# A sum of two accumulator halves: copied half by half, or copied whole and added in SBUF

## The chip, the cores and the metric

The kernel runs on one core of a Trainium2 chip, with its engines TensorE (PE, with its weight loads PEld), VectorE (DVE), ScalarE (ACT), GpSimd (POOL) and the queue of SyncE (SP). The metric is the device time of one execution, in microseconds (us), and the median over the runs is what counts.

## The reference

One decoder block over 256 tokens of width 2048 and 256 memory vectors, all in fp32. Three parts follow one another, each with a norm before and after it and a residual: a mixer of three recurrent branches, a cross attention with 4 heads, and a convolutional FFN.

```python
h = rms_norm(x, norm_mix_pre)
z = h @ w_in                                  # columns of all three branches and their gates
o_a = gated_delta_rule(q, k, v, g, beta)      # 8 heads of 128; q, k, v after a causal conv (4 taps) and silu
y_a = (rms_norm(o_a) * silu(dz)) @ w_dn_out
o_b = gla_chunked(gq, gk, gv, log_a)          # 4 heads, chunks of 64
y_b = (rms_norm(o_b) * silu(gr)) @ w_gla_out
y_s = gelu(s5_ssm(su, ...))                   # 64 groups, state 64, a scan over the tokens
y_c = glu_a * sigmoid(glu_b)                  # glu_a, glu_b = split(y_s @ w_s5_glu)
x = x + rms_norm((g_a * y_a + g_b * y_b + g_c * y_c) @ w_mix_out)
x = x + rms_norm(cross_attention(rms_norm(x), rms_norm(mem)))
gate, up = split(rms_norm(x) @ w_ffn_up)      # 2 x 5632 columns
x = x + rms_norm((gelu(causal_conv(gate)) * up) @ w_ffn_down)
```

## The kernel before

**Products in high and low halves.** Every fp32 operand is split into a rounded half (high) and the rest (low), and a product is made of three passes: high by high, high by low, low by high. `load_w` (lines 199 to 207) loads a weight tile of two 128-row blocks and 512 columns (`raw`, SP's queue), ScalarE casts it to `whi` (L206), and VectorE subtracts to get `wlo` (L206 too). `raw` has four buffers, `whi` and `wlo` three each, so the casts run at most three weight tiles ahead of TensorE.

**Two ways of multiplying.** `proj` keeps features on the partitions: the activations hold their high half in columns 0 to 255 and their low half in columns 256 to 511, so one matmul of 512 columns with `whi` (L222) makes two of the three products side by side in one PSUM bank, and one of 256 columns with `wlo` (L226) adds the third into the first half. A slab is 512 columns of weights, with four accumulators and eight weight tiles for K = 2048. At its end each accumulator holds two halves that have to be added: this is `total` (lines 209 to 213), which the evacuation function of a slab calls for each accumulator. There are 152 such calls: 8 for the S5 input, 24 for the DeltaNet q, k and v, 8 for GLA's q and k, 16 for the two output gates (`gated`), 8 in the cross attention, and 88 in the FFN's upward product. `proj_tok` keeps tokens on the partitions, with two accumulators (L282, L286) and no `total`.

**PSUM.** Five of the eight banks rotate as accumulators (`ps_acc`), three as small tiles (`ps_mx`). A slab of four accumulators therefore begins with one free bank, and its second to fourth accumulators need the banks that the slab before has just filled.

**Rows.** `total` and the evacuations work in rows of 256 columns from a pool (`row`, tag `r1`, 8 buffers in the mixer); rows of 512 columns (`row2`, tag `r2`, 2 buffers) hold the mixer's gates, which go out to DRAM by DMA from GpSimd's queue. In the convolutions (`conv_silu`) the sum is read by ScalarE (L386) and three times by VectorE (L388), in the gates (`gated`) by ScalarE (L626), in the FFN by VectorE's product with the norm and then by ScalarE (L1447) and VectorE (L1449).

**What sets the order.** The Python code emits slabs in order and, between weight tiles, pieces of background work from generators (`pump`): the DeltaNet core, GLA, the S5 expansions (L921), its scan of three small VectorE operations per token (L931 to L933) and its outputs (L946). A scheduler then places all instructions on their engines by its own timeline; `load_w` stands in a high priority. Each engine executes its queue in the order so made, and a change of one helper moves what surrounds it.

Of the kernel before, what the change touches and what calls it, by code (L numbers as in the profile page):

```python
# [9 lines left out]
F32 = mybir.dt.float32  # L10
# [8 lines left out]
P = 128  # L19
T = 256  # L20
# [3 lines left out]
NW = 512  # L24
# [64 lines left out]
class Net:  # L89
# [117 lines left out]
        return hi, lo  # L207

    def total(self, acc, out=None):
        r = self.row() if out is None else out  # L210
        self.nc.scalar.copy(r, acc[:, T:2 * T])  # L211
        self.nc.vector.tensor_add(r, r, acc[:, 0:T])  # L212
        return r

    def tile_passes(self, accs, hi, lo, rhs, g, KT, n):
# [94 lines left out]
    def open_main(self):  # L310
        c = self.ctx
        self.main_stack = ExitStack()
        self.sp = self.main_stack.enter_context(self.pool("sp"))
        self.s16 = self.main_stack.enter_context(self.pool("s16", bufs=1))
        self.s8 = self.main_stack.enter_context(self.pool("s8", bufs=3))
        self.s4 = self.main_stack.enter_context(self.pool("s4", bufs=6))
        self.t1 = self.main_stack.enter_context(self.pool("t1", bufs=8))
        self.jv = self.sp.tile([P, P], F32, name="jv")
        self.ja = self.sp.tile([P, T], F32, name="ja")

# [10 lines left out]
        return self.t1.tile([P, T], F32, name="r1", tag="r1")  # L331

    def row2(self):
        return self.t1.tile([P, NW], F32, name="r2", tag="r2", bufs=2)

    def small_cols(self, small, ab_in):
        nc = self.nc
# [1235 lines left out]
```

## Time and profile before

| | us |
|---|---|
| median of 3 runs | 1924.62 |
| lowest and highest run | 1921.52, 1929.48 |
| the profiled execution | 1925.81 |
| its span, first to last instruction | 1924.0 |
| TensorE busy | 1873.0 |
| VectorE busy | 1415.4 |
| ScalarE busy | 959.6 |

TensorE's mean granted clock over the span is 0.991 of full speed. In the profile, a group of instructions is written as line, engine, operation, output and inputs, shape and count, then the busy time in us, the mean of one in ns, and the engine's idle time before them with what ended it. In a table of stretches, each engine has its busy time and its number of instructions, in the order PE, PEld, DVE, ACT, POOL; then come the granted clock, the DMA's share and GB/s. In a list of waits, a row gives the waiting engine with its tile and line, what it waited for, the sum in us, how often, and the longest. In the timeline, a row starts with its start and duration, and a bracket holds the idle time of the engine before it.

The program begins with the S5 input, then DeltaNet's k, q and v with their convolutions (to about 240 us), the mixer's gates with the DeltaNet core behind them, GLA's q, k and v (about 430 to 545), the DeltaNet gate (from 545), the other gates, the output products and the mix, the cross attention (about 1060 to 1160), and from about 1200 the FFN.

### The profile page before, as it was taken

The page shows a single profiled execution, that of the slowest core. Times are in us where ns is not written, and L with a number is a line of the kernel's source. Part 1 is how long each engine was busy: PE and PEld are TensorE (multiplying, and loading weights), DVE is VectorE, ACT ScalarE, POOL GpSimd, SP SyncE. Part 2 cuts the span into 40 slices and gives each one's busy share as a digit, 9 for nine tenths or more (in the row PEclk, how much of TensorE's full clock was granted, in tenths as well). Part 3 has the DMA queues.
Part 4 walks back from the last instruction along what each step waited for, and adds up shares of the span by engine and source line. Part 5 has one row for each costly group of instructions (what it writes and reads, how often), then busy time and mean ns, then how long its engine had stood idle before and what let it go on. Part 6 is the DMA issues. An engine that isn't in the chain of part 4 may idle for free.

```text
span 1924.0 us, 28133 instructions
## 1 busy us (share of the span) xinstructions
PE 1873.0 (97%) x10440; PEld 1573.9 (82%) x10440; DVE 1415.4 (74%) x2719; ACT 959.6 (50%) x1428; POOL 67.4 (4%) x117
## 2 busy tenths in 40 slices
PE   7999999999999999999999997999999999999997
PEld 6788888777877688888888986888888888888886
DVE  6878999997469999977666755777666677644445
ACT  5655544443564444444455654655555555544442
POOL 0000012020000000000000000000000000000000
PEclk9989999999999999999999998999999999999999
DMA  7544477674445575666587544766666656766664
GB/s 256 164 130 155 155 210 234 195 253 140 133 121 162 182 225 177 213 216 216 186 266 225 174 153 140 219 182 184 201 188 188 189 183 186 228 215 198 198 195 131
DMA packets 107482, 363.93 MB, mean 189 GB/s; under 512 B 12320, under 2 KB 20896, under 8 KB 106832
## 3 DMA queue, kind: packets, MB, share of 16 engines
q1 hardware_dynamic: 97696, 328.32, 55.3%
q0 software_dynamic: 9648, 33.81, 5.3%
q8 instruction: 82, 1.34, 0.3%
q14 instruction: 56, 0.46, 0.1%
HBM read 350.47 MB, written 11.61 MB: 188 GB/s over the span
## 4 chain that ended last, share of the span: by engine, by line
PE 89%; DVE 6%; ACT 2%; issue 1%; DMA 1%; DVEq 0%; SPq 0%; POOL 0%; ACTq 0%; POOLq 0%
PE acc L282 28%; PE acc L222 27%; PE acc L286 14%; PE acc L226 14%; DVE wlo L206 2%; PE mx L921 2%; DMA raw<-in 1%; ACT whi L206 1%; DVE r L388 1%; PE mx L183 0%; PE mx L640 0%; DVE mm L931 0%; DVE f L518 0%; PE mx L946 0%; DVE X L933 0%
## 5 line engine op out<-in xcount | busy, mean ns | idle before, releaser
L206 DVE TENSOR_TENSOR wlo<-raw,whi 128x1024 fp32r<-128x1024 f32 (+1 forms) x632 | 752.3, 1195 | 388.3 <-ACT whi L206 366.6
L206 ACT CAST whi<-raw 128x1024 fp32r<-128x1024 f32 (+1 forms) x632 | 645.6, 1029 | 672.1 <-PE acc L282 339.1
L222 PE MATMUL acc<-aa,whi 128*128 128x512 f32 x2224 | 620.7, 398 | 10.7 <-DVE r L212 8.3
L222 PEld LDWEIGHTS acc<-aa,whi 128*128 128x128 f32 x2224 | 383.6, 190 | 63.9 <-issue 9.8
L226 PEld LDWEIGHTS acc<-aa,wlo 128*128 128x128 f32 x2224 | 345.4, 191 | 59.1 <-DVE wlo L206 11.5
L226 PE MATMUL acc<-aa,wlo 128*128 128x256 f32 x2224 | 362.1, 283 | 7.6 <-DVE wlo L206 7.4
L282 PE MATMUL acc<-whi,aa 128*128 128x512 f32 (+1 forms) x1408 | 346.5, 383 | 0.0
L282 PEld LDWEIGHTS acc<-whi,aa 128*128 128x128 f32 x1408 | 255.3, 188 | 53.3 <-issue 2.3
L286 PE MATMUL acc<-wlo,aa 128*128 128x512 f32 (+1 forms) x704 | 191.5, 383 | 2.8 <-DVE wlo L206 2.7
L286 PEld LDWEIGHTS acc<-wlo,aa 128*128 128x128 f32 x704 | 127.9, 188 | 31.5 <-DVE wlo L206 6.6
L282 PE MATMUL acc<-whi,ach 128*128 128x512 f32 x352 | 137.0, 389 | 0.0
L282 PE MATMUL acc<-whi,acl 128*128 128x512 f32 x352 | 136.9, 389 | 0.0
L931 DVE TENSOR_TENSOR mm<-M,X 128x128 f32<-128x128 f32 x254 | 98.7, 389 | 5.1 <-ACT X L925 0.3
L286 PE MATMUL acc<-wlo,ach 128*128 128x512 f32 x352 | 95.4, 389 | 0.0
L282 PEld LDWEIGHTS acc<-whi,ach 128*128 128x128 f32 x352 | 66.1, 188 | 13.7
L286 PEld LDWEIGHTS acc<-wlo,ach 128*128 128x128 f32 x352 | 66.1, 188 | 13.7
L282 PEld LDWEIGHTS acc<-whi,acl 128*128 128x128 f32 x352 | 66.0, 188 | 13.7
L933 DVE TENSOR_TENSOR X<-X,s__868 128x64 f32<-128x64 f32 x255 | 71.6, 281 | 4.8
L282 PE MATMUL acc<-whi,mgx 128*128 128x512 f32 x256 | 64.3, 391 | 0.1
L211 ACT COPY r<-acc 128x256 f32<-128x256 f32 x143 | 49.6, 362 | 27.3 <-PE acc L222 26.8
L932 DVE TENSOR_TENSOR s__868<-mm 128x64 f32<-128x64 f32 x255 | 56.5, 222 | 4.5
L212 DVE TENSOR_TENSOR r<-r,acc 128x256 f32<-128x256 f32 x143 | 57.0, 413 | 0.9 <-ACT r L211 0.9
(439 smaller groups left out, 1558.5 us busy)
## 6 DMA issues: line engine op xcount, KB each, us to landing
raw<-in SPq DMA_DIRECT2D x600, 512.0 KB, 4.0
raw<-in SPq DMA_DIRECT2D x32, 256.0 KB, 2.7
gd<-r POOLq DMA_DIRECT2D x24, 256.0 KB, 4.4
f<-gd POOLq DMA_DIRECT2D x12, 512.0 KB, 4.8
f<-Rd POOLq DMA_DIRECT2D x4, 512.0 KB, 7.2
f<-in POOLq DMA_DIRECT2D x4, 512.0 KB, 4.5
gp<-in POOLq DMA_DIRECT2D x8, 256.0 KB, 4.7
xn<-in POOLq DMA_DIRECT2D x1, 2048.0 KB, 11.0
```

Source lines behind the costliest of these rows:

```text
L206: self.last = (nc.scalar.copy(hi, raw), self.seq(lambda: nc.vector.tensor_sub(lo, raw, hi.bitcast(F32))))
L211: self.nc.scalar.copy(r, acc[:, T:2 * T])
L212: self.nc.vector.tensor_add(r, r, acc[:, 0:T])
L222: nc.tensor.matmul(accs[m], hi[:, kk, ms[m]], xs[kk].rearrange("p c s -> p (c s)"), start=ks[kk] == 0, stop=ks[kk] == KT - 1)
L226: nc.tensor.matmul(accs[m][:, :T], lo[:, kk, ms[m]], xs[kk][:, 0, :], start=False, stop=False)
L282: nc.tensor.matmul(accs[t], xs[kk][i][:, t * P:(t + 1) * P], hi[:, kk, :], start=ks[kk] == 0 and i == 0, stop=False)
L286: last[:] = [nc.tensor.matmul(accs[t], xs[kk][0][:, t * P:(t + 1) * P], lo[:, kk, :], start=False, stop=ks[kk] == KT - 1)]
L388: nc.vector.scalar_tensor_tensor(c[:, d:], raw[:, :T - d], w[:, j, 3 - d:4 - d], c[:, d:], op0=ALU.mult, op1=ALU.add)
L921: nc.tensor.matmul(ps[:, n, c, :], self.Bl[c][rs, ft, :], su[rs, ft, tk], start=True, stop=True, tile_position=(32 * q, 0))
L931: nc.vector.tensor_mul(m, self.M, prev[:, None].broadcast_to([P, 2, 2, 32]))
L932: nc.vector.tensor_add(s, m[:, :, 0, :], m[:, :, 1, :])
L933: nc.vector.tensor_add(X[:, :, :, t], X[:, :, :, t], s)
```

## The change

`total` copies the whole accumulator, 512 columns, into a row of 512, and VectorE adds the row's two halves in SBUF. Before, ScalarE copied the second half alone and VectorE added the first half to it out of PSUM. Rows of 512 get three buffers in place of two, and the mixer's rows of 256 six in place of eight. The pools of the cross attention and of the FFN, which had no rows of 512, now hold three of them too.

```diff
     def total(self, acc, out=None):
-        r = self.row() if out is None else out
-        self.nc.scalar.copy(r, acc[:, T:2 * T])
-        self.nc.vector.tensor_add(r, r, acc[:, 0:T])
+        both = self.row2()
+        self.nc.scalar.copy(both, acc)
+        r = both[:, :T] if out is None else out
+        self.nc.vector.tensor_add(r, both[:, :T], both[:, T:])
         return r
...
-        self.t1 = self.main_stack.enter_context(self.pool("t1", bufs=8))
+        self.t1 = self.main_stack.enter_context(self.pool("t1", bufs=6))
...
     def row2(self):
-        return self.t1.tile([P, NW], F32, name="r2", tag="r2", bufs=2)
+        return self.t1.tile([P, NW], F32, name="r2", tag="r2", bufs=3)
```

No line on the order of the passes is changed. The scheduler makes a new order from it, though: on TensorE the high passes of a weight tile now stand more often in one run of eight, with the eight low ones behind them. Below `L212` the changed kernel's line numbers are larger by one (its add is L213). Three places of the new order matter further on.

**First place: the first slab of the DeltaNet gate, ScalarE and VectorE.** `r_5473` and its like are rows, `acc` an accumulator, `f_5634` and `f_5711` tiles of GLA. ScalarE before:

```order
L206 CAST whi<-raw 128x1024 x2
L211 COPY r_5473<-acc 128x256
L206 CAST whi<-raw 128x1024
L704 ACTIVATE f_5634<-f_5634 128x1024
L704 ACTIVATE f_5711<-f_5711 128x1024
L626 ACTIVATE r_5472<-r_5473 128x256
L628 ACTIVATE r_5477<-r_5472 128x256
L211 COPY r_5481<-acc 128x256
L626 ACTIVATE r_5480<-r_5481 128x256
L628 ACTIVATE r_5485<-r_5480 128x256
L211 COPY r_5503<-acc 128x256
```

And now:

```order
L206 CAST whi<-raw 128x1024 x2
L211 COPY r_5477<-acc 128x512
L211 COPY r_5485<-acc 128x512
L211 COPY r_5507<-acc 128x512
L206 CAST whi<-raw 128x1024
L705 ACTIVATE f_5638<-f_5638 128x1024
L705 ACTIVATE f_5715<-f_5715 128x1024
L627 ACTIVATE r_5476<-r_5477 128x256
L206 CAST whi<-raw 128x1024 x2
L629 ACTIVATE r_5481<-r_5476 128x256
L627 ACTIVATE r_5484<-r_5485 128x256
L211 COPY r_5515<-acc 128x512
```

The first three copies stand in a row, ahead of GLA's exponentials, and the fourth behind three more casts. VectorE's adds before:

```order
L701 TENSOR_TENSOR f_5711<-f_5258 128x512
L702 TENSOR_TENSOR f_5711<-f_5258 128x512
L212 TENSOR_TENSOR r_5473<-r_5473,acc 128x256
L721 COPY_PREDICATED f_5291<-cst,mx 128x512
L206 TENSOR_TENSOR wlo<-raw,whi 128x1024
```

And now:

```order
L702 TENSOR_TENSOR f_5715<-f_5262 128x512
L703 TENSOR_TENSOR f_5715<-f_5262 128x512
L213 TENSOR_TENSOR r_5477<-r_5477 128x256
L213 TENSOR_TENSOR r_5485<-r_5485 128x256
L213 TENSOR_TENSOR r_5507<-r_5507 128x256
L722 COPY_PREDICATED f_5295<-cst,mx 128x512
L206 TENSOR_TENSOR wlo<-raw,whi 128x1024
```

Three adds stand where one stood, and none of them reads an accumulator.

**Second place: GLA's q and k, ScalarE and TensorE.** `r_4559` to `r_4571` are the rows of q's four accumulators, `f_4305` the buffer that L1182 scales them into, which the DeltaNet core reads until it is done; L587, L604 and L617 are parts of that core. ScalarE before:

```order
L211 COPY r_4559<-acc 128x256
L211 COPY r_4563<-acc 128x256
L211 COPY r_4567<-acc 128x256
L206 CAST whi<-raw 128x1024
L211 COPY r_4571<-acc 128x256
L587 COPY f_3901<-mx 128x512
```

And now, eight casts (one slab) later than there:

```order
L206 CAST whi<-raw 128x1024
L588 COPY f_4137<-mx 128x512
L1183 ACTIVATE f_4305<-r_4559 128x256
L1183 ACTIVATE f_4305<-r_4563 128x256
L1183 ACTIVATE f_4305<-r_4567 128x256
L211 COPY r_4571<-acc 128x512
L605 COPY f_2160<-mx 128x512
```

The fourth copy has moved from the end of q's slab to the end of k's. TensorE at the end of k's slab, before (L282 and L286 are the passes of the v product, L577 to L602 the core's):

```order
L577 MATMUL mx<-f_3757,f_837 64x128 x8
L226 MATMUL acc<-aa,wlo 128x256 x2
L222 MATMUL acc<-aa,whi 128x512
L282 MATMUL acc<-whi,aa 128x512 x4
L286 MATMUL acc<-wlo,aa 128x512 x2
L282 MATMUL acc<-whi,aa 128x512 x4
L286 MATMUL acc<-wlo,aa 128x512 x2
L584 MATMUL mx<-f_2160,f_3467 64x128 x8
L599 MATMUL mx<-f_3757,f_837 64x128 x2
L282 MATMUL acc<-whi,aa 128x512 x4
L286 MATMUL acc<-wlo,aa 128x512 x2
L602 MATMUL mx<-f_4137,f_2583 64x128 x2
```

And now:

```order
L227 MATMUL acc<-aa,wlo 128x256 x2
L223 MATMUL acc<-aa,whi 128x512
L578 MATMUL mx<-f_3757,f_837 64x128 x8
L585 MATMUL mx<-f_2160,f_3467 64x128 x8
L600 MATMUL mx<-f_3757,f_837 64x128 x2
L603 MATMUL mx<-f_4137,f_2583 64x128 x2
```

The three batches of v passes are gone from between the core's products; the first v pass now stands behind all of them and behind the S5 products that follow.

**Third place: the second slab of the DeltaNet gate, TensorE.** L640 are the products that scale the core's output, L718 GLA's level products, one level in each run of 16; `mx` is a small PSUM tile. Before:

```order
L640 MATMUL mx<-r_5518,f_2160 128x64 x8
L718 MATMUL mx<-f_5416 64x64 x16
L222 MATMUL acc<-aa,whi 128x512 x8
L226 MATMUL acc<-aa,wlo 128x256 x8
L222 MATMUL acc<-aa,whi 128x512 x4
L718 MATMUL mx<-f_5553 64x64 x16
L718 MATMUL mx<-f_5634 64x64 x16
L222 MATMUL acc<-aa,whi 128x512 x4
L226 MATMUL acc<-aa,wlo 128x256 x8
L718 MATMUL mx<-f_5711 64x64 x16
```

And now:

```order
L641 MATMUL mx<-r_5522,f_2160 128x64 x8
L719 MATMUL mx<-f_5420 64x64 x16
L227 MATMUL acc<-aa,wlo 128x256 x2
L223 MATMUL acc<-aa,whi 128x512 x2
L719 MATMUL mx<-f_5557 64x64 x16
L719 MATMUL mx<-f_5638 64x64 x16
L719 MATMUL mx<-f_5715 64x64 x16
L719 MATMUL mx<-f_4305 64x64 x16
L227 MATMUL acc<-aa,wlo 128x256 x2
```

The level products have come together, in the last weight tile of the slab, where they were spread over three tiles.

## The prediction

> **What bounds the kernel now.** I read the page's first part, then the waits of TensorE, then the engines by stretches of the program, then the timeline where the longest waits lie.
>
> ```profile
> PE 1873.0 (97%) x10440; PEld 1573.9 (82%) x10440; DVE 1415.4 (74%) x2719; ACT 959.6 (50%) x1428; POOL 67.4 (4%) x117
> ...
> 240.00:432.00 192.00, 189.24 (x1047) 153.31 (x1046) 186.37 (x393) 83.85 (x100) 31.48 (x54) 1.00 0.73 223
> ...
> 584.00:816.00 232.00, 232.00 (x1336) 188.10 (x1337) 221.16 (x542) 111.22 (x163) 10.89 (x18) 1.00 0.63 195
> ...
> 1200.00:1680.00 480.00, 479.72 (x2739) 419.96 (x2738) 338.14 (x542) 260.51 (x403) 1.27 (x2) 1.00 0.63 194
> ```
>
> TensorE (PE, first pair of busy time and count in each stretch) is busy 97% of the span, and from 1200 to 1680 us, the upward FFN product, it idles 0.28 us. All of its passes stay, so nothing is to be had there: 88 of the 152 calls of `total` lie in that product. The gain can only be what TensorE still waits for, 51 us in all, or what it loses at half clock. Its waits name the accumulator:
>
> ```profile
> PE acc L222 <- DVE r L212: 8.3, 5, 2.5
> PE acc L226 <- DVE wlo L206: 7.7, 8, 2.9
> ...
> PE acc L222 <- DVE s__868 L932: 1.7, 3, 1.3
> ```
>
> A first pass into an accumulator (L222) waits for the add in `total` (L212), since that add is the last reader of an earlier accumulator in the same bank. The third row is the same wait under another name: at its longest, the add ends 0.15 us before TensorE goes on.
>
> ```profile
> 197.25 0.41 DVE L212 TENSOR_TENSOR r<-r,acc 128x256 f32<-128x256 f32 x1
> ...
> 197.81 0.70 PE L222 MATMUL acc<-aa,whi 128*128 128x512 f32 x2 [1.26 <-DVE s__868 L932]
> ```
>
> So 8.3 + 1.7 = 10.0 us are spent waiting for that add. Half of it lies in one place, the first slab of the DeltaNet gates:
>
> ```profile
> 569.59 0.37 ACT L211 COPY r<-acc 128x256 f32<-128x256 f32 x1 [3.50 <-PE acc L222]
> ...
> 574.81 0.41 DVE L212 TENSOR_TENSOR r<-r,acc 128x256 f32<-128x256 f32 x1
> ...
> 575.28 0.73 PE L222 MATMUL acc<-aa,whi 128*128 128x512 f32 x2 [2.45 <-DVE r L212]
> ...
> 576.65 0.35 ACT L211 COPY r<-acc 128x256 f32<-128x256 f32 x1
> ...
> 579.82 0.41 DVE L212 TENSOR_TENSOR r<-r,acc 128x256 f32<-128x256 f32 x1
> ...
> 580.38 0.70 PE L222 MATMUL acc<-aa,whi 128*128 128x512 f32 x2 [2.50 <-DVE r L212]
> ```
>
> The copy is done at 569.96, but the add stands in VectorE's queue behind GLA work and starts 4.9 us later. The next accumulator's copy stands on ScalarE behind the first one's gate, and the second wait follows. TensorE then loses time a second way, its granted clock (the number behind the last engine's pair):
>
> ```profile
> 116.00:120.00 4.00, 3.19 (x21) 2.23 (x21) 4.00 (x5) 1.51 (x3) 0.00 (x0) 1.00 0.67 178
> 120.00:124.00 4.00, 4.00 (x26) 3.55 (x25) 2.75 (x6) 2.38 (x5) 0.00 (x0) 0.55 0.67 221
> 124.00:128.00 4.00, 4.00 (x14) 3.16 (x14) 1.41 (x4) 1.67 (x4) 0.00 (x0) 0.50 0.00 0
> 128.00:132.00 4.00, 4.00 (x18) 3.60 (x19) 1.21 (x5) 1.64 (x4) 0.00 (x0) 0.50 0.00 0
> 132.00:136.00 4.00, 4.00 (x19) 3.38 (x19) 3.48 (x19) 1.21 (x3) 0.00 (x0) 0.75 0.01 2
> ...
> 580.00:584.00 4.00, 3.62 (x14) 2.95 (x16) 3.86 (x15) 2.19 (x6) 0.00 (x0) 0.65 0.00 1
> 584.00:588.00 4.00, 4.00 (x38) 3.54 (x38) 3.01 (x8) 2.45 (x4) 0.00 (x0) 0.93 0.02 4
> ```
>
> Around 120 the loss is (0.45 + 0.50 + 0.50 + 0.25) x 4 = 6.8 us; after the two gate waits it is (0.35 + 0.07) x 4 = 1.7 us.
>
> **The change, part by part.** What it does to the instructions is told by these rows:
>
> ```profile
> L212 DVE TENSOR_TENSOR r<-r,acc 128x256 f32<-128x256 f32 x143 | 57.0, 413 | 0.9 <-ACT r L211 0.9
> L211 ACT COPY r<-acc 128x256 f32<-128x256 f32 x143 | 49.6, 362 | 27.3 <-PE acc L222 26.8
> L1443 DVE TENSOR_TENSOR r<-r,rfr 128x256 f32<-128x256 f32 x88 | 35.1, 420 | 0.7
> L1154 ACT ACTIVATE r<-acc 128x512 f32<-128x512 f32 x24 | 14.1, 594 | 11.1 <-PE acc L286 11.1
> ```
>
> *The copy* doubles to 512 columns: the nearest row with that shape out of PSUM is L1154, 594 ns, so 152 x (594 - 362) = 35 us more on an engine that is 50% busy. In the FFN stretch above ScalarE idles 219 of 480 us, and the 88 copies there add 20: nothing. *The add* now reads SBUF only: L1443 has this shape, 420 against 413 ns, so 1 us over 152 calls, hidden in the same way. *The release*: the bank is free when ScalarE has copied, and VectorE's queue no longer stands between. At the gate slab the three first copies now stand in a row (first place of the order above); the one that TensorE wants at 572.83 would end at 569.59 + 0.59 = 570.2. In the convolution slabs the same: -10.0 us, bounds -5 (the half before 240 us is given back, see the rivals) and -10. *The clock* after the gate waits goes with them: -1.7, bounds 0 and -1.7.
>
> *The stretch at half clock around 120.* Ahead of it stand short waits, then the S5 expansions (L921), small products between the passes.
>
> ```profile
> 99.90 0.70 PE L222 MATMUL acc<-aa,whi 128*128 128x512 f32 x2 [1.07 <-DVE r L212]
> ...
> 118.03 0.51 PE L226 MATMUL acc<-aa,wlo 128*128 128x256 f32 x2 [0.65 <-DVE wlo L206]
> ```
>
> The expansions' number stays, their neighbours change. Bounds 0 and -6.8. The trace's other short falls cost 1.7 us; if what stays lies midway between 1.7 and 6.8, it costs 4.3, so -2.5. [...]
>
> *The rows.* The copy now takes a row of 512 columns, of which there are three, shared with the gates' rows. At GLA's q and k (second place) the first three rows are held until the DeltaNet core has left the buffer that L1182 writes; the fourth copy, 8 casts later now, keeps the bank that the v product needs.
>
> ```profile
> 472.53 1.08 PE L282 MATMUL acc<-whi,aa 128*128 128x512 f32 x4
> 473.90 1.07 PE L282 MATMUL acc<-whi,aa 128*128 128x512 f32 x4
> 475.36 1.09 PE L584 MATMUL mx<-f,f 64*64 64x128 f32 x16
> 476.74 1.20 PE L282 MATMUL acc<-whi,aa 128*128 128x512 f32 x4
> ...
> 480.65 1.34 ACT L1182 ACTIVATE f<-r 128x256 f32<-128x256 f32 x4 [3.57 <-PE mx L599]
> ...
> 486.35 1.20 PE L282 MATMUL acc<-whi,aa 128*128 128x512 f32 x4
> ```
>
> Three batches of v passes run here before L1182 can, each 1.37 us from start to start (472.53 to 473.90): 4.1 us of work that now waits. Without them the core's own products move up: L584's input is ready some 1.8 us before it runs, and what follows it is held by the third batch for about 1 us more, so about 2.7. So +1.4 us, bounds 0 and +4.1.
>
> *GLA's level products* (third place) now come in one block behind the gates' products, which hold two of the three small PSUM tiles until their rows are ready.
>
> ```profile
> 592.21 0.74 DVE L721 COPY_PREDICATED f<-cst,mx 128x512 f32<-128x512 int32 x1
> 592.83 1.23 DVE L727 TENSOR_TENSOR f<-f 128x1024 f32<-128x1024 f32 x1
> ...
> 593.54 2.09 PE L718 MATMUL mx<-f 128*64 128x64 f32 x64
> ```
>
> Each needs the tile that an L721 frees. Two L721 and the L727 between them are 2.7 us of VectorE against the 2.1 us of two levels on TensorE (these 64 instructions): about 0.6, and a little more at the transposes behind; I take +1.0, bounds 0 and +4, a wait of this size at each of the last levels.
>
> The profiled execution took 1925.81 us, 1.8 beyond its span of 1924.0, and 1.2 above the median of 1924.62. Sum: 1925.8 - 10.0 - 1.7 - 2.5 + 1.4 + 1.0 = 1914.0, and 1.2 less against the median: **1913 us**, 0.6% faster.
>
> **The rivals.** *The half-clock stretch stays whole*, or comes at another place: 1913 + 2.5 to 4 = 1916 to 1917. For it: the L921 are all still there. *It is gone*, because the waits for the add ahead of it are gone as they are in the gate slab: 1913 - 4.3 = 1909. For it: the fall at 580 came right after two such waits. Against it: the 1.07 us lies 20 us ahead of this one, and the wait for wlo at 118 stays. [...]
>
> *The wait becomes one for the low halves.* VectorE is busy 186 of 192 us from 240 and 221 of 232 from 584; if TensorE comes earlier, it may wait there for wlo, as it already does for 7.7 us. Then the 5 us before 240 and some of the gate's 5 come back, and the clock loses as before: 1922 to 1924, no change. Against it: VectorE has 5.6 and 10.8 us to spare there, and TensorE had no wait at all from 584 to 816.
>
> *Slower: the fourth copy blocks ScalarE.* With three rows for four accumulators, the fourth copy waits for the first row, and the casts of the weights stand behind it in ScalarE's queue.
>
> ```profile
> 1316.38 0.48 DVE L1449 SCALAR_TENSOR_TENSOR r<-r,vec,r 128x254 f32<-128x254 f32 x1
> ...
> 1317.98 0.36 ACT L211 COPY r<-acc 128x256 f32<-128x256 f32 x1
> ...
> 1320.04 2.00 ACT L206 CAST whi<-raw 128x1024 fp32r<-128x1024 f32 x2 [0.60 <-PE acc L222]
> ```
>
> Today the first row's last reader ends at 1316.86, 1.1 us ahead of the fourth copy, and the next cast still waits 0.6 us for TensorE, two weight tiles ahead (5.6 us: a tile is 16 passes, and 2739 passes fill the 480 us above). It decides from about 5 us of delay a slab; 1 us beyond that in 20 FFN slabs would make 1913 + 20 = 1933.
>
> **How the numbers follow.** The forecast (1908 to 1918 with its own spread) 0.42; stretch whole or elsewhere 0.20; stretch gone 0.18; waits for wlo 0.12; slower 0.08. A measurement can tell 0.5%, 9.6 us, so faster means below 1915.0: 0.29 of the first, 0.06 of the second, all of the third, 0.53, and 0.01 from the fourth. Slower by over 0.5% comes from the last, 0.08, and 0.01 from the fourth; no change is the rest, 0.37. Range: the lower end is all bounds at their best, 1925.8 - 18.5 - 1.2 = 1906, and 2 of the 7.7 us for wlo, 1904; the upper end takes in the fourth case, 1923.
>
> **What would show it.** Right: no row "PE acc <- DVE" for the add, and less than 2 us for the copy in its stead; L211 at about 590 ns and its add at about 420; no wait and full clock in the gate slab; 1 to 4 us of new idle time before the v product; the FFN still without idle time. Wrong: more than 8 us for wlo, a half-clock stretch of 7 us or more, or waits of "ACT r L211" for VectorE followed by late casts.

## The result: 1909 us, 0.85% faster

| | before | after |
|---|---|---|
| median of 4 runs, us | 1926.27 | 1909.32 |
| lowest and highest | 1921.52, 1929.48 | 1908.72, 1909.99 |
| the profiled execution, its span | 1925.81, 1924.0 | 1909.99, 1907.8 |
| TensorE busy, idle in the span | 1873.0, 51.0 | 1863.1, 44.7 |

The ratio of the runs is 0.9915, with an interval of 0.9902 to 0.9929. The forecast was 1913 us, with a range of 1904 to 1923 and 0.54 for faster by over 0.5%. Time and direction came out inside it, but two terms of the sum were wrong in size, on opposite sides, and what one of them was taken from differs from one execution to the next.

In the profile after, the waits of TensorE come first. A row gives the waiting engine with its tile and line, what it waited for, the sum in us, how often, and the longest.

```profile
PE acc L223 <- DVE xset L1061: 10.6, 2, 10.2
PE acc L227 <- DVE wlo L206: 6.9, 5, 2.9
PE mx L183 <- DVE xn L1289: 5.9, 1, 5.9
PE acc L287 <- DVE wlo L206: 3.2, 8, 0.8
PE mx L947 <- issue: 1.8, 1, 1.8
PE mx L585 <- DVE f L580: 1.3, 1, 1.3
PE mx L922 <- DVE rsoy L196: 0.9, 1, 0.9
PE mx L719 <- DVE f L722: 0.7, 1, 0.7
```

The waits for the add (8.3 and 1.7 us before) are gone, and none for the copy stands in their place. Waits for the low halves are 6.9 us on L227, 7.7 before on the same line; they did not take over. Four new rows stand at L947, L585, L922 and L719. The groups show what the copy and the add cost now (busy us, mean ns, idle time before them):

```profile
L211 ACT COPY r<-acc 128x512 f32<-128x512 f32 x151 | 87.0, 582 | 35.4 <-PE acc L223 28.0 <-DVE f L1090 0.5
L213 DVE TENSOR_TENSOR r<-r 128x256 f32<-128x256 f32 x144 | 59.9, 420 | 4.8 <-ACT r L211 4.4
```

The copy takes 582 ns (the estimate was 594), the add 420 (420). By stretches of the profile after, with the busy time and count of PE, PEld, DVE, ACT and POOL, then the granted clock:

```profile
0.00:240.00 240.00, 227.44 (x1353) 197.54 (x1354) 204.29 (x512) 146.45 (x226) 5.70 (x13) 0.99 0.60 186
432.00:488.00 56.00, 51.73 (x462) 40.95 (x459) 45.78 (x128) 26.37 (x57) 2.09 (x4) 0.97 0.39 116
545.00:640.00 95.00, 94.06 (x715) 72.20 (x714) 91.85 (x208) 52.81 (x86) 5.43 (x8) 1.00 0.53 164
...
56.00:60.00 4.00, 4.00 (x18) 3.39 (x18) 4.00 (x8) 3.55 (x8) 0.00 (x0) 0.69 0.72 240
...
120.00:124.00 4.00, 4.00 (x33) 3.28 (x32) 2.79 (x5) 2.57 (x7) 0.00 (x0) 1.00 0.84 233
124.00:128.00 4.00, 4.00 (x33) 3.62 (x32) 2.99 (x7) 3.67 (x8) 0.00 (x0) 1.00 0.39 160
...
580.00:584.00 4.00, 4.00 (x38) 3.36 (x38) 3.90 (x9) 1.64 (x2) 0.00 (x0) 1.00 0.67 207
...
1200.00:1680.00 480.00, 480.00 (x2720) 420.41 (x2719) 334.52 (x522) 274.46 (x393) 1.27 (x2) 1.00 0.66 197
```

And the first three stretches in the profile of before, for comparison:

```profile
0.00:240.00 240.00, 219.99 (x1274) 188.38 (x1275) 195.37 (x505) 133.44 (x212) 5.71 (x13) 0.97 0.54 172
432.00:488.00 56.00, 55.96 (x540) 43.50 (x539) 42.57 (x118) 24.37 (x61) 1.56 (x3) 1.00 0.40 123
545.00:640.00 95.00, 90.06 (x695) 73.27 (x694) 87.46 (x188) 51.57 (x76) 2.74 (x4) 0.98 0.48 147
```

TensorE's idle time falls from 20.0 to 12.6 us up to 240 us and from 4.9 to 0.9 us around the DeltaNet gate, and it rises from 0.04 to 4.3 us at GLA's q and k (432 to 488). The clock is full behind 120 and behind the gate's products. It is new at half from 55 to 58 us, after a wait of 2.01 us for a low half at 54.62, and at 471 us, behind the new idle time. The FFN has no idle time, as before. From first to last, the idle time fell by 6.3 us (51.0 to 44.7) and the time lost at half clock before TensorE's end by about 5.1 (13.6 to 8.5, half of the length of the stretches at half clock in each profile); together 11.4 of the 15.8 us between the two profiled executions. The other 4.4 are taken up further on.

Four questions were left: which part of the program makes the gain, whether the pools or the copy make it, what the new idle time at GLA's q and k hangs on, and whether the change had really removed the stretch at half clock around 120 us.

### The profile page after: what moved, and what is told of

The parts are those of the page before. It is cut to its first block, busy times and chain, and to the rows that moved or that the text cites. A ratio compares the mean times of both kernels' runs of the same rounds, so it can differ in the third digit from the quotient of the medians.

```text
span 1907.8 us, 28125 instructions
## 1 busy us (share of the span) xinstructions
PE 1863.1 (98%) x10440; PEld 1569.4 (82%) x10440; DVE 1418.0 (74%) x2719; ACT 985.1 (52%) x1426; POOL 67.4 (4%) x117
## 4 chain that ended last, share of the span: by engine, by line
PE 72%; DVE 2%; DMA 1%; issue 0%; ACT 0%; DVEq 0%; ACTq 0%
PE acc L283 25%; PE acc L223 21%; PE acc L287 12%; PE acc L227 11%; PE mx L922 1%; DVE wlo L206 1%; PE mx L183 1%; DMA raw<-in 1%; PE mx L641 0%; PE mx L754 0%; DVE aa L1478 0%; PE mx L757 0%; PE mx L764 0%; PE mx L947 0%; PE mx L1372 0%
## 5 line engine op out<-in xcount | busy, mean ns | idle before, releaser
L223 PE MATMUL acc<-aa,whi 128*128 128x512 f32 x2224 | 604.9, 395 | 0.8 <-DVE aa L1297 0.4
L223 PEld LDWEIGHTS acc<-aa,whi 128*128 128x128 f32 x2224 | 387.6, 189 | 57.3 <-issue 1.2
L227 PEld LDWEIGHTS acc<-aa,wlo 128*128 128x128 f32 x2224 | 334.4, 190 | 47.6 <-DVE wlo L206 6.8
L227 PE MATMUL acc<-aa,wlo 128*128 128x256 f32 x2224 | 350.3, 283 | 4.9 <-DVE wlo L206 4.9
L283 PE MATMUL acc<-whi,aa 128*128 128x512 f32 (+1 forms) x1408 | 346.9, 384 | 0.0
L283 PEld LDWEIGHTS acc<-whi,aa 128*128 128x128 f32 x1408 | 255.5, 188 | 53.9 <-issue 2.6
L283 PE MATMUL acc<-whi,ach 128*128 128x512 f32 x352 | 136.9, 389 | 0.0
L283 PE MATMUL acc<-whi,acl 128*128 128x512 f32 x352 | 136.9, 389 | 0.0
L211 ACT COPY r<-acc 128x512 f32<-128x512 f32 x151 | 87.0, 582 | 35.4 <-PE acc L223 28.0
L283 PEld LDWEIGHTS acc<-whi,acl 128*128 128x128 f32 x352 | 66.0, 188 | 13.7
L283 PEld LDWEIGHTS acc<-whi,ach 128*128 128x128 f32 x352 | 66.1, 188 | 13.7
L283 PE MATMUL acc<-whi,mgx 128*128 128x512 f32 x256 | 64.2, 390 | 0.0
L213 DVE TENSOR_TENSOR r<-r 128x256 f32<-128x256 f32 x144 | 59.9, 420 | 4.8 <-ACT r L211 4.4
```

The costliest lines, as they stand in the source:

```text
L211: self.nc.scalar.copy(both, acc)
L213: self.nc.vector.tensor_add(r, both[:, :T], both[:, T:])
L223: nc.tensor.matmul(accs[m], hi[:, kk, ms[m]], xs[kk].rearrange("p c s -> p (c s)"), start=ks[kk] == 0, stop=ks[kk] == KT - 1)
L227: nc.tensor.matmul(accs[m][:, :T], lo[:, kk, ms[m]], xs[kk][:, 0, :], start=False, stop=False)
L283: nc.tensor.matmul(accs[t], xs[kk][i][:, t * P:(t + 1) * P], hi[:, kk, :], start=ks[kk] == 0 and i == 0, stop=False)
```

## The experiments

### Early part and late part

`total` gets a flag, so that a part of the program can use the old two instructions. The pools are those of the change.

```diff
 def total(self, acc, out=None):
+    if not getattr(self, "whole", True):
+        r = self.row() if out is None else out
+        self.nc.scalar.copy(r, acc[:, T:2 * T])
+        self.nc.vector.tensor_add(r, r, acc[:, 0:T])
+        return r
     both = self.row2()
...
     dn = n.spawn(n.dn_core(), R_DN)
+    n.whole = False
```

This is b_early: the whole copy up to DeltaNet's v, the old total behind it. In c_late the flag is False from the start and True from the same place on.

> The whole copy only in the S5 input and in DeltaNet's k, q and v; from the first gate slab on the old total, with the pools of the change. Theory (the first 280 us gained 16.7 us, and behind them gain and loss cancel): about 1909 us, no add waits before 240 us, the two waits of 2.5 us and 1.7 us of half clock back in the DeltaNet gate, no new idle time ahead of the v product. Rival (the gain comes evenly with the number of calls, 40 of 152 here): about 1921 us.

> The opposite: the old total up to DeltaNet's v, the whole copy from there on. Theory: the add waits of the first 240 us (5 us shown) and the stretch at half clock stay, the gate slab gains 6 us and GLA's q and k lose 6 us: 1925 us, no change. Rival (even gain by calls, 112 of 152): about 1914 us. If the pool sizes or the new order alone had made the gain of the first 240 us, it would be there in this run too: about 1910 us.

b_early took 1912.49 us, a ratio of 0.994 (0.9927 to 0.9952); c_late 1920.9 us, 0.9975 (0.9965 to 0.9986). The two gains are about 11.6 and 4.8 us of the 1925.05 that the kernel before took beside them, and the ratios multiply to 0.9915, the whole change. The early part has 32 of the 152 calls (8 for the S5 input, 24 for DeltaNet's q, k and v) and the late part 120, where the expectations say 40 and 112. So 32 calls have most of the gain, and the rival of an even gain falls: it wanted 1921 and 1914, with the right counts about 1922 and 1912. b_early is 3.5 us above the 1909 expected, its profiled execution (1911.23) 1.2 above that of the change; its waits in the gate slab are back, with 2.45 and 0.95 us, and so is the half clock there. Ahead of the v product it loses 1.6 us (0.32 and 1.23), where none was expected. But the part behind 280 us is not the tie that the theory made of it. The waits of TensorE in c_late show why:

```profile
PE acc L228 <- DVE r L213: 3.4, 3, 1.5
...
PE mx L724 <- DVE f L727: 0.9, 1, 0.9
PE mx L927 <- ACT f L610: 0.7, 1, 0.7
```

The add waits of the first part stand (3.4 us, and 1.7 under the other name); those of the gate slab are gone. At GLA's q and k, however, c_late loses 1.2 us (0.7 here, and two shorter waits of 0.26 and 0.32), not the 4.3 us of the change, and no row for the S5 outputs (L952 in its numbers) appears. The whole loss needs both, the late copies and a TensorE that arrives early: c_late has the first alone, b_early the second alone, and each loses less than half of it. The clock, too, came out otherwise: 3.3 us lost around 120 in place of 6.6 (below).

e_pools is the kernel before with two numbers altered:

```diff
-self.pool("t1", bufs=8)
+self.pool("t1", bufs=6)
...
-name="r2", tag="r2", bufs=2
+name="r2", tag="r2", bufs=3
```

> The kernel before with the pools of the change alone (six rows of 256, three of 512), total as it was. Theory (the whole copy makes the gain): the add waits of about 10 us stay, 1922 to 1928 us. Rival (pool sizes and the order that follows from them): clearly faster, 1910 to 1918 us.

1925.72 us, ratio 1.0005 (0.999 to 1.002), and the waits as they were:

```profile
PE acc L222 <- DVE r L212: 8.3, 5, 2.5
...
PE acc L222 <- DVE s__868 L932: 1.7, 3, 1.3
```

The pools alone change nothing that can be measured.

### What holds GLA's k and v

In the change, q's sums take the three rows of 512. This is TensorE, then VectorE and ScalarE there in the profile after:

```profile
455.00 1.09 PE L578 MATMUL mx<-f,f 128*64 128x128 f32 x16
457.40 1.09 PE L585 MATMUL mx<-f,f 64*64 64x128 f32 x16 [1.31 <-DVE f L580]
...
461.37 0.44 PE L603 MATMUL mx<-f,f 64*64 64x128 f32 x4
463.61 3.70 PE L947 MATMUL mx<-X,f 128*32 128x128 f32 x128 [1.80 <-issue]
467.24 1.15 PE L922 MATMUL mx<-f,bl 32*128 32x128 f32 x8
469.25 1.12 PE L922 MATMUL mx<-f,bl 32*128 32x128 f32 x8 [0.86 <-DVE rsoy L196]
470.31 2.80 PE L283 MATMUL acc<-whi,aa 128*128 128x512 f32 x8
...
463.23 0.27 DVE L934 TENSOR_TENSOR X<-X,s__868 128x64 f32<-128x64 f32 x1
...
461.49 1.03 ACT L1183 ACTIVATE f<-r 128x256 f32<-128x256 f32 x3 [2.38 <-PE mx L600]
462.43 0.56 ACT L211 COPY r<-acc 128x512 f32<-128x512 f32 x1
```

No v pass (L283) runs before 470.31. L1183 empties q's rows only from 461.49 on, since it waits for the core's last product (L600); the copy at 462.43 is q's fourth, and those of k begin behind it, at 463.37. So far this is the step as predicted. What was not seen is how much then shows: with no v passes between them, the core's products wait for VectorE (1.31 at L585), and the S5 outputs (L947) wait for the scan, whose last step ends at 463.50. TensorE comes to these outputs 17 us earlier than in the profile of before (463.61 against 480.90), and the scan ends only 1.3 us earlier (463.50 against 464.79).

d_gq lets q alone take the old total, in rows of 256:

```diff
+n.whole = False
 section("gq", 1, ...)
+n.whole = True
```

> The change, but GLA's q takes the old total, so its four sums stand in rows of 256 and the three rows of 512 are free for GLA's k. Theory (the q sums hold the rows of 512 until the DeltaNet core leaves its buffer, so k's banks stay full and the v product stands behind): the batches of v passes run among the core's last products again, the 4.2 us of new idle time and the 1.7 us of half clock at 471 us go, about 1904 us. Rival (the new idle time comes from the core's end, which the scan on VectorE delays whatever the rows do): 1908 to 1910 us, idle time as in the change.

1903.34 us, a ratio of 0.9895 (0.988 to 0.991). TensorE, then ScalarE at the same place in its profile (its lines are larger by five):

```profile
460.34 1.89 PE L288 MATMUL acc<-whi,aa 128*128 128x512 f32 x7
...
462.97 1.98 PE L288 MATMUL acc<-whi,aa 128*128 128x512 f32 x8
...
475.86 3.70 PE L952 MATMUL mx<-X,f 128*32 128x128 f32 x128
...
457.16 0.57 ACT L216 COPY r<-acc 128x512 f32<-128x512 f32 x1
...
475.61 1.34 ACT L1189 ACTIVATE f<-r 128x256 f32<-128x256 f32 x4 [2.52 <-PE mx L605]
```

k is copied at once behind its passes, 18 us before L1189 empties q's rows; the v product runs in whole batches of eight between the core's products, where before it had batches of four; no wait over 0.2 us is left there, and the S5 outputs find the scan done. Between 432 and 488 us TensorE has no idle time, and the rival falls, that the scan sets this time whatever the rows do. That d_gq is faster than the change is likely and not certain: its interval ends at 0.991, that of the change begins at 0.9902.

f_four asks the same by another way: one row of 512 more.

```diff
-self.pool("t1", bufs=6)
+self.pool("t1", bufs=4)
...
-name="r2", tag="r2", bufs=3
+name="r2", tag="r2", bufs=4
```

> The change with four rows of 512 and four of 256 in place of three and six. Theory (three rows for the four q sums are what held GLA's banks): with a fourth row q's four copies leave their banks at once, v passes run ahead of the core's last products again, the new idle time of 4.3 us there falls below 2 us, 1903 to 1906 us. Rival (rows of 512 are not the limit, or four rows of 256 are too few for the convolutions): 1909 us or more, with waits of the copies or for wlo in the first 240 us.

Here both sides were half right. In the q and k region 1.3 us of idle time are left (0.32 and 0.96), below the 2 us expected. But the kernel took 1912.45 us, 0.9934 (0.9919 to 0.995). A part of that stands far ahead, TensorE first, then VectorE:

```profile
121.60 2.08 PE L227 MATMUL acc<-aa,wlo 128*128 128x256 f32 x8 [5.88 <-DVE wlo L206]
...
118.05 1.23 DVE L893 TENSOR_TENSOR f<-f,bl 128x1024 f32<-128x1024 f32 x1 [10.80 <-DMA f<-zd]
...
120.33 1.22 DVE L206 TENSOR_TENSOR wlo<-raw,whi 128x1024 fp32r<-128x1024 f32 x1
```

In the order made from these pool sizes, whose passes differ from those of the change from 42 us on, a step of the S5 setup (L893) stands on VectorE ahead of a weight tile's low half, and it waits 10.8 us for a DMA. Everything behind it waits too. In the change the same step waits 0.3 us, at 105.5: its DMAs were issued 8 us earlier there (from 95.6, here from 103.5) and landed in at most 7.8 us, here in up to 12.5. That the four rows of 256 moved them was not shown; any other new order might have done it.

### The stretch at half clock

In the profile after, the stretch around 120 us is gone, which the prediction had given 0.18. Was that the change? The kernel before was profiled again, unaltered, as a_again.

> The kernel before once more, for a second profile of it. If the stretch at half clock belongs to the program's order (the S5 expansions and the 0.8 us of waits just ahead of it, which do not change), it stands again at 120 to 134 us with 6.8 us lost, and the waits for the add sum to 10 us again. If it is an accident of one execution, the granted clock stays full from 116 to 136 or falls elsewhere, and the span differs by up to 7 us from 1924.0.

1928.23 us, and neither side of the expectation quite. The waits ahead stand as they were, and there are falls of the clock, but at other times and in another number. One row each for the same 55 us, in a_again:

```profile
110.00:165.00 55.00, 54.07 (x309) 45.33 (x308) 35.28 (x83) 26.23 (x45) 0.00 (x0) 0.84 0.36 107
```

and in c_late, whose passes have the same order here:

```profile
110.00:165.00 55.00, 54.04 (x335) 45.79 (x333) 39.84 (x94) 28.12 (x48) 0.00 (x0) 0.94 0.39 119
```

That is (1 - 0.84) x 55 = 8.8 us lost in one and 3.3 in the other, with the same waits ahead. So the times at which the clock falls and rises were read in stretches of 0.5 us, for instance in the profile of before:

```profile
120.00:120.50 0.50, 0.50 (x10) 0.50 (x10) 0.50 (x1) 0.36 (x2) 0.00 (x0) 0.88 0.96 393
120.50:121.00 0.50, 0.50 (x7) 0.50 (x5) 0.50 (x3) 0.44 (x1) 0.00 (x0) 0.50 0.71 287
...
581.00:581.50 0.50, 0.50 (x4) 0.45 (x3) 0.50 (x3) 0.39 (x2) 0.00 (x0) 0.68 0.00 0
```

The clock falls at 120.5 - 0.12 = 120.38 and at 581.5 - 0.32 = 581.18. All falls and rises of one execution, worked out in this way, lie on a grid of 3.413 us to within 0.02 us: from 120.38 to 581.18 is 135 times that, to 1164.86 another 171, to 1192.16 eight more, and each stretch at half clock lasts one, two, three or four times that. The grid's phase is another in each execution: the falls leave 0.91 us when divided by 3.413 in the profile of before, 2.11 in a_again, 0.46 in that of after, 0.99 in c_late. Over all 14 profiles, some 7,600 stretches of this grid at full clock, 51 were followed by half clock. What these have in common is what TensorE did in them. Where only idle time lowers it, the clock fell behind every stretch with a busy time of up to 1.47 us of the 3.41 (without the first 15 us of the program, in which passes take twice their time although the view gives 1.00: eight of L222 take 3.75 us at 10.14 in the profile of before, and 2.02 at 15.03). S5 expansions counted for less: in ten stretches the clock fell behind a TensorE that was never idle, and all ten hold 2.31 us of expansions or more. One of them in c_late, first all of TensorE's work, then the expansions alone (L927 in its numbers, 32 partitions of 128):

```profile
120.46:123.87 3.41, 3.41 (x33) 3.03 (x33) 2.71 (x6) 2.66 (x7) 0.00 (x0) 1.00 0.70 229
123.87:127.28 3.41, 3.41 (x12) 2.80 (x12) 2.22 (x6) 1.66 (x4) 0.00 (x0) 0.50 0.13 50
...
120.46:123.87 3.41, 2.91 (x30) 2.53 (x29) 1.00 0.70 229
```

With the expansions counted at a quarter, one rule holds both kinds in these profiles: work of 1.50 us or less in a stretch always brought half clock in the next, 1.87 or more never did, and between the two both occur. The quarter is an estimate, a number that fits these 51 falls; no kernel was made to measure it, nor to tell whether the 32 rows of the expansions or something else about them makes them count for less. The first stretch at half clock in the profile of before has both causes in the stretch ahead of it:

```profile
116.97:120.38 3.41, 2.60 (x20) 1.75 (x19) 3.41 (x4) 1.50 (x4) 0.00 (x0) 1.00 0.74 232
```

It holds 0.8 us of waits (0.65 of them for a low half at 118.03) and 1.21 us of expansions, which leaves 1.69 us of work by the rule; with either alone it would be about 2.5.

i_spread puts this to use, on the kernel with the old total for q: the first 16 groups of expansions are asked for more slowly.

```diff
-yield 1.0 * QB
+yield (1.3 if hf == 0 else 1.0) * QB
```

> The kernel with the old total for GLA's q, and the first 16 groups of S5 expansions asked for every 1.9 weight tiles in place of every 1.4, so that fewer stand in one heap. Theory (a grid of 3.41 us, its phase drawn anew by each execution, halves the clock for a stretch when the one before it holds so many expansions of 32 rows that TensorE's work, with these counted at a quarter, is below about 1.7 us): no half clock between 110 and 170 us whatever the phase, 1900 us, and the runs within 3 us of each other where they spread over 7 us. Rival (the falls come from the waits ahead of the expansions, or from something other than their heap): the same falls in about half of the executions, 1903 us, and the spread as before.

> The kernel with the spread expansions once more. Theory: full clock from 110 to 170 us at another phase of the grid too. Rival (its first profile was a lucky phase, as that of the change was): a stretch at half clock there.

> The same, a third profile. Theory: full clock from 110 to 170 us. Rival: a stretch at half clock there in this profile or in the one before it.

k_thin does it on the kernel before, where all waits for the add stay ahead of the expansions:

```diff
-yield 1.0 * QB
+yield (2.4 if hf == 0 and f2 < 2 else 1.0) * QB
```

> The kernel before, with nothing changed except that the first eight groups of S5 expansions are asked for every 3.4 weight tiles in place of every 1.4. All waits for the add ahead of them stay (96 and 100 us). Theory (the expansions' heap makes the half clock, the waits do not): no half clock between 110 and 170 us, 1918 to 1921 us, and less spread than before. Rival (the waits for the add make it): half clock as before in some executions, 1925 us.

And the change itself was profiled twice more.

> The changed kernel once more, for a second profile. Theory (the half clock behind the S5 expansions is drawn by the phase of the 3.41 us grid, and the change leaves heaps of 24 and 16 expansions): unless the phase is again near that of the first profile, one or more stretches of 3.4 us at half clock stand between 110 and 165 us. Rival (the change has removed the stretch, because no add wait stands ahead of it any more): none, in this profile and the next.

> The same, a third profile. Theory: of the two new profiles at least one has a stretch at half clock between 110 and 165 us. Rival: none.

The time lost from 110 to 165 us, from one such row of each profile as (1 - clock) x 55:

| order of the expansions | profiles | lost, us |
|---|---|---|
| as before | before, a_again, e_pools, c_late | 6.6, 8.8, 3.3, 3.3 |
| as in the change | after, after_2, after_3, b_early, d_gq | 0, 1.7, 6.6, 0, 6.6 |
| spread | i_spread, i_spread_2, i_spread_3 | 0, 0, 0 |
| own order, with the wait of 5.88 us | f_four | 8.8 |
| thinned, waits kept | k_thin | 0 |

The rows of after_3:

```profile
110.00:165.00 55.00, 55.00 (x328) 47.01 (x327) 34.81 (x88) 30.64 (x51) 0.00 (x0) 0.88 0.38 112
```

of i_spread_2:

```profile
110.00:165.00 55.00, 55.00 (x359) 47.93 (x359) 42.49 (x93) 34.59 (x57) 0.00 (x0) 1.00 0.48 146
```

and of k_thin:

```profile
110.00:165.00 55.00, 54.31 (x341) 47.20 (x340) 46.33 (x98) 31.79 (x53) 0.00 (x0) 1.00 0.52 164
...
PE mx L946 <- issue: 13.6, 1, 13.6
```

after_3 has no idle time of TensorE in these 55 us, and its clock falls as before; it took 1916.10 us, after_2 1910.04. k_thin has the waits for the add (0.79 us at 96.72, 1.07 at 100.12) and full clock. So these waits are neither needed for this stretch nor enough; the heap of expansions makes it, by the phase of the execution. How much of the full clock is luck can be estimated: the grid was laid over the traces of after, i_spread and k_thin at 86 phases, and the stretch with the least work by the rule sought between 110 and 165 us. By the phase this is 1.27 to 1.72 us in the change, 1.72 to 2.24 in i_spread, and 1.42 to 2.13 in k_thin, where 6 phases in 10 come below 1.70. No stretch with expansions and more than 1.70 us of work by the rule was followed by half clock in these profiles, so i_spread should keep the clock at any phase, while k_thin's one profile, and the first one of the change, may well be lucky draws. The change's own executions differ by them: five of six lie from 1908.7 to 1910.0, and one at 1916.1.

In time, neither kernel gained what was expected. k_thin took 1937.19 us, 1.0064 (1.0043 to 1.0085): with thinner expansions the scan begins at 203 us in place of 159 and ends at 872 in place of 816, so that the S5 outputs (L946) keep TensorE idle for 13.6 us at 858, with half clock behind it (0.86 from 840 to 900, 8.4 us). i_spread took 1903.11 us, 0.9881 (0.9862 to 0.99), as d_gq did within what can be told, and its runs spread from 1899.9 to 1905.7, where 3 us were expected. Its three profiles took 1899.93, 1900.33 and 1903.29 us, against 1906.97 for that of d_gq. What moves the others is open; its waits of 1.99 us at 55 and of 2.92 us at 1166 are near the bound as well, and a phase decides on them.

## Why the prediction held, step by step

**The waits for the add, -10.0.** Gone, all of them, in the change and in each part that takes the whole copy. But a wait cost more than the idle time that its row shows. In the profile of before:

```profile
98.43 0.40 PE L226 MATMUL acc<-aa,wlo 128*128 128x256 f32 x2
99.90 0.70 PE L222 MATMUL acc<-aa,whi 128*128 128x512 f32 x2 [1.07 <-DVE r L212]
100.44 0.40 PE L226 MATMUL acc<-aa,wlo 128*128 128x256 f32 x2
```

A run of eight low passes takes 0.95 us from its start to the next, so by this estimate two are over at 98.67, and the next pass starts at 99.90: 1.23 us, not 1.07, which the row counts from the end that it shows for the pair, 98.83. The first pair behind the wait then takes 0.54 us, the following ones 0.47. That is some 0.2 to 0.3 us beside each wait, and the other waits of over 0.25 us in this profile give the same sum (0.16 us up to the next pass, 0.07 to 0.1 in it). The change has 12 fewer waits of over 0.15 us, of all kinds, up to 240 us, and six more than before between 240 and 640, so this makes 1 to 2 of the 4.4 us that idle time and clock leave over. The rest was not traced. This is the first mis-sized term: -10.0 was the idle time, not the price.

**The clock behind the gate waits, -1.7.** Right: from 576 to 588 us the clock is full.

**The stretch around 120, -2.5.** In the compared profiles it was -6.8, the whole bound. But the step that failed is its premise, that a stretch is a property of the kernel which the change keeps, moves or removes. How much of it comes is drawn by each execution (3.3 to 8.8 us in the four profiles of the old order, 0 to 6.6 in the five of the new one); the prediction took one draw for the rule. One of its signs of being wrong, a half-clock stretch of 7 us or more, is absent from the first profile of the change and present in after_3 (10.2 us from 134.4 on), so it could not tell. Over the profiles of the table the old order lost 5.5 us on average and the new one 3.0, so the -2.5 is near the mean, by no merit of its working. The rival "it is gone" met the first profile, for a reason that is refuted: the waits for the add ahead.

**GLA's q and k, +1.4.** Right in place and mechanism, wrong in size: 4.2 us of idle time more, and 1.7 us at half clock in this execution (in after_2 and after_3 the waits are the same, and the clock stays full). The step that failed is that the core's products would move up when the v passes are away. They wait for VectorE instead, and the S5 outputs for the scan, since TensorE comes 17 us earlier and the scan 1.3. The upper bound, +4.1, was the better value.

**GLA's level products, +1.0.** 0.7 us (L719 for L722). Right.

**FFN, +0.** No idle time, with 88 of the longer copies. The slower rival, copies that wait for a row and hold the casts, did not occur there. Where rows did hold copies, at GLA's k, no cast was late by it that TensorE waited for.

**What was not in the sum.** The second S5 input slab now waits 2.01 us for a low half at 54.62, against three shorter waits before, of 1.5 us together. It costs little itself, but its stretch of the grid held only 1.4 us of work, and the clock fell behind it.

So -11.8 was forecast and -15.8 measured between the profiled executions. The sum left out 4.3 us at the stretch, the 4.4 us beside idle time and clock, and 2.3 us of other waits in the first 240 us that went too, for low halves and at L397; that the adds no longer stood in VectorE's way at the same moments may be why, and was not traced. It was too good by 4.5 us at GLA's q and k, by the 1.7 us at 55 us, and by 0.9 us of small waits elsewhere. Four of these six were in no term; that the total came near is partly luck.

## What to carry to other kernels

Here an accumulator that two engines had to read came free when the slower queue got to it, and TensorE waited 10.0 us for that in all. One whole copy by the engine with the shorter queue (ScalarE, busy 52% of the span) took these waits away, and doubling it, from 362 to 582 ns, cost TensorE no idle time in the FFN, where ScalarE was busy 274 of 480 us. The row that takes the copy then becomes the thing that is held, so count for each place how long its reader holds it, and let a place with a late reader keep the old form (here worth 4 us by the ratios, 6 by the medians, with intervals that just overlap). Before a gain or loss is put down to the clock, profile the same kernel twice: a stretch at half clock may be a draw (0, 1.7 and 6.6 us lost there in three profiles of the change).

## What the runs showed of the hardware that was not expected

- In the 14 profiles the granted clock changed only on a grid of 3.413 us, whose phase was constant within an execution (to 0.02 us) and another in each (0.91 us in the profile of before, 2.11 in a_again, with the same kernel).
- Half clock came with TensorE never idle, behind small products on 32 of 128 partitions: 2.31 us or more of them in a stretch of 3.41 brought it in ten cases; 2.26 us and less never did where TensorE was busy throughout, and between 2.30 and 2.36 three kept the clock. Whether the 32 partitions are the reason was not tested by itself.
- A wait of TensorE cost 0.2 to 0.3 us beyond the idle time that its row shows (at 99.90 in the profile of before 1.23 for 1.07 us, and 0.54 for 0.47 in the pair behind it).
